# Half-block products of a SwiGLU block: token sums on VectorE, the norm hooks one step sooner, four split columns ahead of the last block product

## The chip, the cores and the metric

The kernel runs on one core of a Trainium2 chip. TensorE (PE) does the matrix products, VectorE (DVE), ScalarE (ACT) and GpSimd (POOL) the elementwise work, SyncE (SP) and GpSimd issue transfers. The metric is device microseconds of one execution; three runs of the kernel before were timed.

## The reference, cut to what matters

Two layers work on 512 tokens of width 1024 in float32. Layer 0 mixes tokens with a convolution module, layer 1 with native sparse attention; each mixer is followed by a SwiGLU feed-forward block, and the change lies in that block alone:

```python
h = rmsnorm(x, norm_ffn[i])                      # x: 512 tokens x 1024
gate, up = jnp.split(h @ w_in, 2, axis=-1)       # w_in: 1024 x 2*2816
x = x + (jax.nn.silu(gate) * up) @ w_out         # w_out: 2816 x 1024
```

## The kernel before, in words

Activations lie transposed: eight tiles `x[0..7]` of 128 channels x 512 tokens. Every float32 product is made of three rounded ones: each operand is split into a high part and a remainder, and PE computes high x high, low x high and high x low (L255, L256, L257 for whole tiles, L773 for half blocks). Weights come as 160 units of at most 128x1024 (`wr`, three buffers). ScalarE rounds a unit into `wh` (L195), VectorE takes the remainder into `wl` (L204); both have two buffers, so unit i+2 is rounded only when PE has used unit i for the last time.

The block (`ffn`, once a layer) has these stages.

- **Start.** Four units (27 to 30 in layer 0) make four projection tiles. The sum of squares over channels was gathered in `acc`; `norm_1` puts it on PE (`ssq`, L315) and takes a reciprocal root on VectorE, `norm_2` spreads it over the partitions (`rbc`, L324) and copies it to `R` (L327). The pair of numbers `FFN_H` says behind which of the eight half-unit steps each hook is written.
- **Whole tiles.** Units 31 to 38 make gate and up of four more tiles of hidden channels; `act` evacuates them (L688 to L692), and `divide` splits the result into `ah` (L673) and `al` (L674). Meanwhile `operand(c)`, c = 0 to 3, prepares the half-block products: the normed tokens of channel tiles c and c+4 go to `z` (L703), four halves of 256 tokens called b11, b12, b21, b22, and from them come four sums t1 to t4 in `zt` (L708 to L711, on GpSimd). All seven blocks are split into `bh` and `bl` (L714 to L718).
- **Pairs.** The other 16 hidden tiles take seven products of half blocks each, instead of eight (`pair`, L773); GpSimd adds the weight sums (L747, L748) and issues their transfers (L736, L740).
- **Output.** `out_mm(m, fs)` multiplies split columns fs of the hidden tiles by the output weights of channel tile m. The units stand in the order (0,0), (1,0), (0,1), (1,1), (0,2), (1,2), (2,0) and so on, tile m and block b of at most eight columns; (0,2) and (1,2) have six columns, so 18 matmuls each. In layer 0 they are units 54 to 59, and (2,0) is unit 60. Behind block 2 of a tile comes its residual add (L920; L925 in layer 1), and in layer 0 its split for the next layer, `hh` on ScalarE (L289) and `hl` on VectorE (L290). The last product of the last pair (`tail(q)`, half block 6) stands among the first `out_mm` calls. It writes over a PSUM half that VectorE reads first (L798, in `finish`).

A scheduler sets the order of each engine's queue from the written order and its own estimate of readiness; queues then run strictly in order. Operations passed to `pe(...)` keep their written order, and so does what goes through `held(...)` while `hold[0]` is true (`w_hi`, `w_lo`, `mm3`, `divide`). `hold` is set before the output stage and, before the change, cleared behind the last product of tile 1.

Of the kernel before, what the change touches and what calls it, by code (L numbers as in the profile page):

```python
# [15 lines left out]
ALU = mybir.AluOpType  # L16
# [4 lines left out]
T = 512  # L21
# [61 lines left out]
Q2B = 3  # L83


FFN_H = (1, 3)
NREG = 6
NST = NF - NREG
NB = 7
# [19 lines left out]
def trunk(ctx: ExitStack, tc: tile.TileContext, A, out):  # L109
    nc = tc.nc  # L110
# [64 lines left out]
    hold = [False]  # L175
# [464 lines left out]
    def ffn(acc, gnext, layer, between=None):  # L640
# [9 lines left out]
        with ExitStack() as cx:  # L650
# [49 lines left out]
            def operand(c):  # L700
                z, zt = (sw.tile([P, 2 * T], F32, tag="gagb"[c % 2 * 2:][:2] + e, name=nm("z")) for e in "hl")
                for i in range(2):
                    nc.vector.scalar_tensor_tensor(z[:, i * T:(i + 1) * T], x[c + 4 * i], v(gcol + c + 4 * i), R,  # L703
                                                   ALU.mult, ALU.mult)
                b11, b12, b21, b22 = (z[:, i * H:(i + 1) * H] for i in range(4))
                t1, t2, t3, t4 = (zt[:, i * H:(i + 1) * H] for i in range(4))
                gp = nc.gpsimd
                gp.tensor_tensor(t1, b11, b12, ALU.subtract)  # L708
                gp.tensor_tensor(t2, t1, b22, ALU.add)
                gp.tensor_tensor(t4, b21, t2, ALU.subtract)  # L710
                gp.tensor_tensor(t3, b12, b22, ALU.subtract)  # L711
                h_ = sb.tile([P, NB * H], F32R, tag=f"bh{c}", name=nm("bh"))
                l_ = sb.tile([P, NB * H], F32R, tag=f"bl{c}", name=nm("bl"))
                nc.scalar.activation(h_[:, :H], b11, AF.Copy, scale=-1.0)  # L714
                nc.vector.scalar_tensor_tensor(l_[:, :H], b11, -1.0, h_[:, :H], ALU.mult, ALU.subtract)
                for d, e in ((slice(H, 3 * H), z[:, T:]), (slice(3 * H, NB * H), zt)):
                    nc.scalar.activation(h_[:, d], e, AF.Copy)
                    nc.vector.tensor_tensor(l_[:, d], e, h_[:, d], ALU.subtract)  # L718
                bh.append(h_)
                bl.append(l_)  # L720
# [46 lines left out]
            def product(ps, w, i, b, first, last):  # L767
                wh, wl = w
                for c in range(4):
                    k = slice(i * T + c * P, i * T + (c + 1) * P)  # L770
                    t = slice(b * H, (b + 1) * H)
                    for q, (p_, m_) in enumerate(((wh, bh), (wh, bl), (wl, bh))):
                        pe(nc.tensor.matmul(ps[:, :H], p_[:, k], m_[c][:, t], start=first and c == 0 and q == 0,  # L773
                                            stop=last and c == 3 and q == 2, skip_group_check=True))
# [25 lines left out]
            def pair(n, prev):  # L800
                q = dict(n=n, a=bank())
                last = n == NST - 1
                w1 = next_w(False)
                product(q["a"], w1, 0, 0, True, True)
                if prev:
                    finish(prev)
                s_g2(n)
                s_acc(n + 2)
                s_add(n + 1)
                s_load(n + 2)  # L810
                s_pre(n + 3)
                q["d"] = bank()
                product(q["d"], part[n, "ga"], 0, 3, True, True)
                c1 = copied(q["a"], "c1")
                post = tail(prev) if prev else None
                q["c5"] = copied(q["d"], "c5")
                if post:
                    post()
                w_hi(state["next"])
                w_lo()  # L820
                product(q["a"], part[n, "ga"], 1, 4, False, True)
                s_part(n, "gc", raw[n])
                b = bank()
                product(b, w1, 1, 1, True, True)
                c2 = copied(q["a"], "c2")
                s_g1(n + 1)
                if last:
                    product(q["a"], part[n, "gb"], 0, 5, False, True)
                product(q["d"], part[n, "gb"], 1, 2, False, True)
                g = q["g"] = ft.tile([P, T], F32, tag="g", name=nm("g"))  # L830
                pe(nc.vector.tensor_tensor(g[:, :H], b[:, :H], c1, ALU.subtract))
                if not last:
                    product(q["a"], part[n, "gb"], 0, 5, False, True)
                pe(nc.vector.tensor_tensor(g[:, H:], q["d"][:, :H], c2, ALU.subtract))
                return q

# [38 lines left out]
                    divide(f, fo)  # L875

            hold[0] = True
            out_mm(0, (0, 1))
            w_hi(state["next"])
            w_lo()  # L880
            finish(q)
            tail(q)()
            out_mm(0, (2, 3))
            sx.close()
            fo = cx.enter_context(tc.tile_pool(name="fo", bufs=1, side="right", reuse_waits="tile"))
            parts(4, 5, 6, 7)
# [16 lines left out]
            out_mm(1, range(8, 16))  # L903
            w_lo()
            parts(19, 20, 21)
            acc = new_acc() if gnext is not None else None
            for m, b in OUT_ORDER[4:]:
                if m not in pss:
# [5 lines left out]
                out_mm(m, range(8 * b, min(8 * b + 8, NF)))  # L914
                if b < 2:
                    continue
                if m == 1:
                    hold[0] = False
                if gnext is not None:
                    nc.vector.tensor_tensor(x[m], x[m], ps, ALU.add)  # L920
                    finish_x(m, gnext, acc, fin(m))
# [847 lines left out]
```

## Time and profile before

| | |
|---|---|
| timed, median of 3 (lowest to highest) | 1284.72 us (1283.82 to 1286.34) |
| the profiled execution, its own time | 1284.19 us |
| its span, first to last instruction | 1282.4 us |
| mean granted TensorE clock | 0.995 |
| feed-forward block of layer 0, from the start | about 199 to 565 us |
| feed-forward block of layer 1 | about 915 us to the end |

All moments are microseconds from the span's start. A row of a timeline gives start, duration, engine, line, operation, output<-inputs, shapes and count; in square brackets stands the idle time of the engine just ahead of it and who ended it. Durations reach past the start of the next operation where an engine overlaps them: matmuls of 512 columns are shown at about 0.39 us and start 0.23 us apart. A row of the view of waits gives total us, times, and the longest.

### The profile page before, as it was taken

What the parts mean: (1) busy time and instruction counts of PE and PEld (TensorE: products, weight loads), DVE (VectorE), ACT (ScalarE), POOL (GpSimd) and SP (SyncE); (2) the same over time, 40 slices, a digit from 0 to 9 for tenths busy, and PEclk for the clock granted to TensorE, in tenths of its full rate; (3) what the DMA queues carried; (4) which work ended last, traced back from release to release, by engine and by line L of the source; (5) the groups of instructions that cost most, each with busy time, mean ns of one, the idle gap of its engine ahead of it and who ended that gap; (6) DMA issues with size and microseconds to landing.
All of it is one profiled execution on the core that took longest, in us unless ns stands there. A gap on an engine that the chain in (4) does not pass through costs nothing.

```text
span 1282.4 us, 20571 instructions
## 1 busy us (share of the span) xinstructions
PE 1231.7 (96%) x7943; PEld 1032.1 (80%) x7943; DVE 817.6 (64%) x1419; ACT 560.8 (44%) x1032; POOL 371.6 (29%) x419
## 2 busy tenths in 40 slices
PE   9999799899999999999998999999989999999998
PEld 6787687689999878887777776667867999997886
DVE  5996475868666544235687777663495877855321
ACT  5322353445555533233344577773344555554211
POOL 2011023425443001121332465651262444420000
PEclk9999999999999999999999899999999999999999
DMA  8758324347776132244255101002443567732331
GB/s 310 255 186 286 84 95 152 98 123 190 192 193 158 50 100 97 91 148 110 72 138 161 25 21 39 1 17 67 148 106 108 157 174 184 197 98 91 111 113 45
DMA packets 81282, 160.03 MB, mean 125 GB/s; under 512 B 36000, under 2 KB 36896, under 8 KB 79648
## 3 DMA queue, kind: packets, MB, share of 16 engines
q1 hardware_dynamic: 65808, 109.07, 27.3%
q0 software_dynamic: 15376, 49.65, 15.1%
q8 instruction: 62, 1.02, 0.3%
q14 instruction: 36, 0.29, 0.1%
HBM read 145.16 MB, written 5.28 MB: 117 GB/s over the span
## 4 chain that ended last, share of the span: by engine, by line
PE 77%; DVE 9%; DMA 3%; POOL 3%; issue 3%; ACT 2%; SPq 1%; DVEq 0%; POOLq 0%; ACTq 0%
PE st L773 25%; PE pp L257 8%; PE pp L255 8%; PE pp L256 8%; PE st L255 6%; PE st L257 6%; PE st L256 6%; PE O L1511 3%; DVE wl L204 2%; PE cpe L466 2%; PE T L1485 1%; DVE Pm L1457 1%; POOL z L708 1%; PE S L1454 1%; DVE t L1488 1%
## 5 line engine op out<-in xcount | busy, mean ns | idle before, releaser
L195 ACT ACTIVATE wh<-wr 128x1024 fp32r<-128x1024 f32 (+3 forms) x160 | 162.4, 1015 | 329.0 <-PE st L256 149.6
L204 DVE TENSOR_TENSOR wl<-wr,wh 128x1024 fp32r<-128x1024 f32 (+3 forms) x160 | 198.3, 1240 | 130.6 <-ACT wh L195 127.3
L257 PE MATMUL pp<-hh,wl 128*128 128x512 f32 x448 | 177.3, 398 | 9.8 <-DVE wl L204 9.8
L773 PE MATMUL st<-bh,sh 128*128 128x256 f32 x640 | 182.3, 285 | 1.3 <-DVE t L798 1.3
L773 PE MATMUL st<-bh,sl 128*128 128x256 f32 x640 | 181.2, 283 | 1.1 <-DVE sl L757 1.1
L255 PE MATMUL pp<-hh,wh 128*128 128x512 f32 x448 | 177.6, 399 | 3.6 <-DVE gr L413 1.9
L773 PE MATMUL st<-bl,sh 128*128 128x256 f32 x640 | 180.7, 282 | 0.0
L256 PE MATMUL pp<-hl,wh 128*128 128x512 f32 x448 | 177.4, 397 | 0.1
L255 PE MATMUL st<-ah,wh 128*128 128x512 f32 x352 | 140.3, 399 | 3.0 <-ACT wh L195 3.0
L256 PE MATMUL st<-al,wh 128*128 128x512 f32 x352 | 140.2, 398 | 0.0
L257 PE MATMUL st<-ah,wl 128*128 128x512 f32 x352 | 139.9, 398 | 0.0
L757 DVE TENSOR_TENSOR sl<-S,sh 128x512 fp32r<-128x512 f32 x128 | 103.9, 848 | 43.0 <-ACT sh L756 41.7
L773 PEld LDWEIGHTS st<-bh,sh 128*128 128x128 f32 x640 | 122.3, 191 | 2.7 <-DVE t L798 2.2
L773 PEld LDWEIGHTS st<-bh,sl 128*128 128x128 f32 x640 | 122.5, 191 | 1.5 <-DVE sl L757 1.5
L773 PEld LDWEIGHTS st<-bl,sh 128*128 128x128 f32 x640 | 122.8, 192 | 0.0
L257 PEld LDWEIGHTS pp<-hh,wl 128*128 128x128 f32 x448 | 84.2, 188 | 33.1 <-DVE wl L204 14.1
L255 PEld LDWEIGHTS pp<-hh,wh 128*128 128x128 f32 x448 | 84.3, 189 | 27.0 <-ACT wh L195 4.2
L256 PEld LDWEIGHTS pp<-hl,wh 128*128 128x128 f32 x448 | 84.4, 188 | 20.5 <-issue 1.1
L1472 POOL TENSOR_SCALAR Pm<-Pm,sm,gates 128x512 f32<-128x512 f32 (+3 forms) x128 | 80.8, 645 | 62.8 <-DVE sm L1468 49.9
L299 POOL TENSOR_TENSOR acc<-acc,sq 128x512 f32<-128x512 f32 x18 | 31.1, 1729 | 212.1 <-ACT sq L297 198.3
L1458 ACT ACTIVATE Pm<-Pm,mx 128x512 f32<-128x512 f32 (+3 forms) x128 | 71.1, 557 | 38.5 <-DVE mx L1457 33.1
L255 PEld LDWEIGHTS st<-ah,wh 128*128 128x128 f32 x352 | 66.7, 190 | 19.8 <-ACT wh L195 3.8
(281 smaller groups left out, 2514.3 us busy)
## 6 DMA issues: line engine op xcount, KB each, us to landing
S<-fw_x POOLq DMA_DIRECT2D x64, 512.0 KB, 5.8
wr<-fw_in SPq DMA_DIRECT2D x48, 512.0 KB
wr<-fw_o SPq DMA_DIRECT2D x32, 512.0 KB
bd<-bands POOLq DMA_DIRECT2D x12, 1280.0 KB, 11.4
r<-fw_x SPq DMA_DIRECT2D x32, 256.0 KB
wr<-cw_in SPq DMA_DIRECT2D x14, 512.0 KB
wr<-fw_o SPq DMA_DIRECT2D x16, 384.0 KB
wr<-fw_s SPq DMA_DIRECT2D x8, 512.0 KB
```

The source lines that it names most:

```text
L195: held(after(nc.scalar.activation(hi[:, :cols], raws[i][:, :cols], AF.Copy), pin.get(AF)))
L204: held(after(nc.vector.tensor_tensor(lo[:, :cols], raws[i][:, :cols], hi[:, :cols], ALU.subtract), pin.get(ALU)))
L255: held(nc.tensor.matmul(ps, wh, xh, start=first, stop=False))
L256: held(nc.tensor.matmul(ps, wh, xl, start=False, stop=False))
L257: held(nc.tensor.matmul(ps, wl, xh, start=False, stop=last))
L299: (eng or nc.gpsimd).tensor_tensor(acc, acc, sq, ALU.add)
L466: last["conv"] = nc.tensor.matmul(ps[e * 64:e * 64 + 16 * m, g, :], w, f[:, g0 + g, 4 - s:68 - s], start=s == 0, stop=s == 4)
L757: pe(nc.vector.tensor_tensor(l_[:, c], z, h_[:, c], ALU.subtract))
L773: pe(nc.tensor.matmul(ps[:, :H], p_[:, k], m_[c][:, t], start=first and c == 0 and q == 0, stop=last and c == 3 and q == 2, skip_group_che ...
L1458: at_[AF] = nc.scalar.activation(Pt, Pt, AF.Exp, bias=mx, scale=-1.0, accum_out=sm)
L1472: nc.gpsimd.tensor_scalar(Pt, Pt, sm[:, k:k + 1], gates[:, t + k, br * 16 + h:br * 16 + h + 1], ALU.mult, ALU.mult)
L1511: pe(nc.tensor.matmul(o[par * 64:par * 64 + 64, P * kc:], vf[br][:, kc, g], Us[par][kc], start=False, stop=last))
```

## The change

- `FFN_H` goes from (1, 3) to (0, 2): both norm hooks are written one half-unit step earlier.
- `operand` computes the sums on VectorE. One 128x512 subtraction makes t1 and t3 (the view takes b11 and b12 from one half, b12 and b22 from the other), then two of 128x256 make t2 and t4. Per block 16 GpSimd operations become 12 VectorE operations. In `zt` t3 now stands second and t2 third, so `pair` names half blocks 4 and 5 the other way round.
- Columns 0 to 3 of output tile 0 are all written ahead of `finish(q)` and the last block product; before, columns 0 and 1 stood ahead and 2 and 3 behind.
- `hold` is cleared ahead of the loop that begins with unit (0,2).

```diff
-FFN_H = (1, 3)
+FFN_H = (0, 2)
...
-                t1, t2, t3, t4 = (zt[:, i * H:(i + 1) * H] for i in range(4))
-                gp = nc.gpsimd
-                gp.tensor_tensor(t1, b11, b12, ALU.subtract)
-                gp.tensor_tensor(t2, t1, b22, ALU.add)
-                gp.tensor_tensor(t4, b21, t2, ALU.subtract)
-                gp.tensor_tensor(t3, b12, b22, ALU.subtract)
+                nc.vector.tensor_tensor(zt[:, :T].rearrange("p (a b) -> p a b", a=2),
+                                        z[:, :T].rearrange("p (a b) -> p a b", a=2),
+                                        z.rearrange("p (a b) -> p a b", a=2)[:, :, H:], ALU.subtract)
+                nc.vector.tensor_tensor(zt[:, T:T + H], zt[:, :H], b22, ALU.add)
+                nc.vector.tensor_tensor(zt[:, T + H:], b21, zt[:, T:T + H], ALU.subtract)
...
-                product(q["a"], part[n, "ga"], 1, 4, False, True)
+                product(q["a"], part[n, "ga"], 1, 5, False, True)
...
-                    product(q["a"], part[n, "gb"], 0, 5, False, True)
+                    product(q["a"], part[n, "gb"], 0, 4, False, True)
...
             hold[0] = True
-            out_mm(0, (0, 1))
+            out_mm(0, range(4))
...
             tail(q)()
-            out_mm(0, (2, 3))
...
             parts(19, 20, 21)
+            hold[0] = False
...
-                if m == 1:
-                    hold[0] = False
```

What this does to the queues is shown at two places of layer 0; layer 1 has the same moves. First VectorE, where the operands begin. `z_2162` is z of c = 0, `z_2163` its sums, `z_2252` before and `z_2251` after are z of c = 1; `wl_2072` is unit 30. Before:

```order
L715 SCALAR_TENSOR_TENSOR bl_2171<-z_2162,bh_2170 128x256
L204 TENSOR_TENSOR wl_2072<-wr_2007,wh_2071 128x1024
L718 TENSOR_TENSOR bl_2171<-z_2162,bh_2170 128x512
L715 SCALAR_TENSOR_TENSOR bl_2261<-z_2252,bh_2260 128x256
L718 TENSOR_TENSOR bl_2261<-z_2252,bh_2260 128x512
L688 TENSOR_TENSOR g_2101<-pp_1950,Rb_2039 128x512
```

Now the same stretch of VectorE's queue; lines behind L706 stand one lower in the changed file (L717 was L718, L714 was L715), and L706, L709 and L710 are the sums.

```order
L714 SCALAR_TENSOR_TENSOR bl_2170<-z_2162,bh_2169 128x256
L706 TENSOR_TENSOR z_2163<-z_2162 128x512
L204 TENSOR_TENSOR wl_2072<-wr_2007,wh_2071 128x1024
L706 TENSOR_TENSOR z_2252<-z_2251 128x512
L717 TENSOR_TENSOR bl_2170<-z_2162,bh_2169 128x512
L714 SCALAR_TENSOR_TENSOR bl_2259<-z_2251,bh_2258 128x256
L717 TENSOR_TENSOR bl_2259<-z_2251,bh_2258 128x512
L709 TENSOR_TENSOR z_2163<-z_2163,z_2162 128x256
L688 TENSOR_TENSOR g_2101<-pp_1950,Rb_2027 128x512
```

The first subtraction stands ahead of the remainder of unit 30, and one more VectorE operation ahead of the first evacuation. Twelve such rows are spread over the stretch, and the 16 rows of L708 to L711 are gone from GpSimd's queue, where the two transfers of L740 stood behind the first two of them. No matmul changes its place in this stage, and the rows of L315, L324 and the root's operations stand where they stood on PE and VectorE.

The second place is the passage from output tile 1 to output tile 2. On PE the numbered names are `wh59` and `wl59` for unit (1,2) and `wh60` for unit (2,0). Before:

```order
L255 MATMUL st_447_4621<-ah_464_4726,wh59_4781 128x512
L256 MATMUL st_447_4621<-al_465_4727,wh59_4781 128x512
L255 MATMUL st_482_4842<-ah_108_2107,wh60_4811 128x512
L256 MATMUL st_482_4842<-al_109_2108,wh60_4811 128x512
L257 MATMUL st_447_4621<-ah_464_4726,wl59_4782 128x512
```

And PE's queue after the change, from the same matmul:

```order
L255 MATMUL st_447_4617<-ah_464_4722,wh59_4777 128x512
L256 MATMUL st_447_4617<-al_465_4723,wh59_4777 128x512
L257 MATMUL st_447_4617<-ah_464_4722,wl59_4778 128x512
L255 MATMUL st_447_4617<-ah_466_4726,wh59_4777 128x512
L256 MATMUL st_447_4617<-al_467_4727,wh59_4777 128x512
```

The two matmuls of unit 60 that stood third and fourth now come behind all 18 of unit 59. ScalarE's queue at that place, before (`hh0` and `acc` read the finished x[0]):

```order
L673 ACTIVATE ah_474_4776<-y_438_4591 128x512
L195 ACTIVATE wh59_4781<-wr59_4696 128x768
L289 ACTIVATE hh0_477_4805<-x0_76,vec_74 128x512
L297 ACTIVATE acc_476_4780<-x0_76 128x512
L195 ACTIVATE wh60_4811<-wr60_4738 128x1024
```

ScalarE's queue after:

```order
L673 ACTIVATE ah_474_4772<-y_438_4593 128x512
L195 ACTIVATE wh59_4777<-wr59_4692 128x768
L195 ACTIVATE wh60_4807<-wr60_4734 128x1024
L289 ACTIVATE hh0_477_4801<-x0_76,vec_74 128x512
L297 ACTIVATE acc_476_4776<-x0_76 128x512
```

Unit 60 is rounded before ScalarE turns to x[0]. On VectorE, in the same way, the remainder of unit 59 now stands ahead of the residual add of x[0] and that of unit 60 right behind it; before, the add and `hl0` stood ahead of both. Outside the block, a few VectorE rows of the attention stage of layer 1 change places: two rows of a softmax (L1284, L1285) and a score row (L1457) of 128x512.

More of the change, by code (lines that the diff above doesn't have):

```diff
@@ L832, in pair @@
                 if not last:
-                    product(q["a"], part[n, "gb"], 0, 5, False, True)
+                    product(q["a"], part[n, "gb"], 0, 4, False, True)
                 pe(nc.vector.tensor_tensor(g[:, H:], q["d"][:, :H], c2, ALU.subtract))
```

## The prediction

> **What bounds the kernel now.** I read the page first, then PE's waits stage by stage, then the timelines of the engines named there. The page's row of busy time:
>
> ```profile
> PE 1231.7 (96%) x7943; PEld 1032.1 (80%) x7943; DVE 817.6 (64%) x1419; ACT 560.8 (44%) x1032; POOL 371.6 (29%) x419
> ```
>
> PE is the bound. The change takes no matmul away, so it can win only what PE idles, or runs slowly, in the two feed-forward blocks. PE's waits in layer 0 from 196 to 280 us, the start and whole-tile stages:
>
> ```profile
> PE pp L257 <- DVE wl L204: 4.7, 4, 1.9
> PE st L773 <- DVE sl L757: 0.5, 1, 0.5
> PE pp L255 <- ACT wh L195: 0.5, 1, 0.5
> ```
>
> Layer 1, asked from 912 to 996 us, answers with the same three rows, so what holds here holds twice. Four waits are for the remainder of a weight unit on VectorE. Why it comes late stands in VectorE's timeline:
>
> ```profile
> 215.83 3.71 DVE L703 SCALAR_TENSOR_TENSOR z<-x,vec,Rb 128x512 f32<-128x512 f32 x4 [2.69 <-ACT Rb L327]
> ...
> 220.34 5.04 DVE L204 TENSOR_TENSOR wl<-wr,wh 128x1024 fp32r<-128x1024 f32 x1
> ...
> 230.30 1.40 DVE L703 SCALAR_TENSOR_TENSOR z<-x,vec,Rb 128x512 f32<-128x512 f32 x2
> ...
> 237.56 0.41 DVE L715 SCALAR_TENSOR_TENSOR bl<-z,bh 128x256 fp32r<-128x256 f32 x1
> 237.89 0.68 DVE L718 TENSOR_TENSOR bl<-z,bh 128x512 fp32r<-128x512 f32 x1
> 238.50 0.68 DVE L692 TENSOR_TENSOR y<-y,g 128x512 f32<-128x512 f32 x1
> 239.10 1.21 DVE L204 TENSOR_TENSOR wl<-wr,wh 128x1024 fp32r<-128x1024 f32 x1
> 240.23 0.41 DVE L715 SCALAR_TENSOR_TENSOR bl<-z,bh 128x256 fp32r<-128x256 f32 x1
> ```
>
> The same remainder takes 5.04 us at 220.34 and 1.21 us at 239.10. The difference is what GpSimd did, in its own timeline:
>
> ```profile
> 221.20 1.72 POOL L708 TENSOR_TENSOR z<-z 128x256 f32<-128x256 f32 x1
> ...
> 235.98 5.87 POOL L708 TENSOR_TENSOR z<-z 128x256 f32<-128x256 f32 x1 [8.88 <-DVE bl L718]
> ```
>
> Its sums ran beside the slow remainder, and when VectorE was dense (236 to 242) the sum itself took 5.87 us. Each slows the other. The late second pair of sums then holds ScalarE, and VectorE behind it:
>
> ```profile
> 246.80 1.06 ACT L717 ACTIVATE bh<-z 128x1024 fp32r<-128x1024 f32 x1 [6.96 <-POOL z L710]
> ```
>
> So all four remainder waits lead back to the GpSimd sums: two through slow or backed-up VectorE work (1.9 and 1.62 us), one small one, and one of 0.79 us behind this hold. Two further places matter at the block's end; their rows stand with their terms.
>
> **The change part by part.** *Operand sums.* First, what the waits cost. PE's timeline, at the stage's start, at the wait that will stay, and at its end, and the groups of that stage:
>
> ```profile
> 214.91 0.48 PE L257 MATMUL pp<-hh,wl 128*128 128x512 f32 x1
> ...
> 239.25 0.50 PE L255 MATMUL pp<-hh,wh 128*128 128x512 f32 x1 [0.50 <-ACT wh L195]
> ...
> 264.38 0.39 PE L257 MATMUL pp<-hh,wl 128*128 128x512 f32 x1
> ...
> 274.14 0.39 PE L257 MATMUL pp<-hh,wl 128*128 128x512 f32 x1
> ```
>
> ```profile
> L257 PE MATMUL pp<-hh,wl 128*128 128x512 f32 x76 | 30.3, 401 | 4.7 <-DVE wl L204 4.7
> L255 PE MATMUL pp<-hh,wh 128*128 128x512 f32 x75 | 29.8, 397 | 0.5 <-ACT wh L195 0.5
> L256 PE MATMUL pp<-hl,wh 128*128 128x512 f32 x75 | 29.6, 395 | 0.0
> ```
>
> From 264.38 to 274.14 PE made 14 steps of three without a wait: 9.76 / 42 = 0.2324 us a matmul. The stage has 76 + 75 + 75 = 226 matmuls, 52.52 us at that rate; it took 274.14 + 0.23 - 214.91 = 59.46 us. So 6.94 us are lost, more than the 5.2 us of shown waits, since each wait also costs the overlap (0.16) and a slow next matmul (0.11). Of the 6.94, 0.09 belongs to the `rbc` matmuls ahead and 0.50 + 0.28 = 0.78 to the wait at 239.25. That one stays: PE's queue keeps one pair of unit 33 ahead of unit 32's third matmul, and `wh` of unit 33 waits for PE's own last use of unit 31. Removable: 6.07 us.
>
> Do the waits go? Twelve operations join VectorE: by the starts above (0.33 from one to the next for 256 columns, 0.60 for 512) four times 0.60 + 2 x 0.33, 5.1 us a block. The cover is PE's 0.23 us a matmul; I laid the new queue out row by row. VectorE starts at 215.83 and waits for nothing before unit 33, the tightest. Ahead of that remainder stand 36 operations: eight L703 (0.665 each, by the pair at 230.30), eight of 256 columns, fifteen of 512, and two splits and three remainders of 1024 (1.13 each), 5.3 + 2.7 + 9.0 + 5.65 = 22.65 us. It starts at about 238.5 and ends at 239.7. PE reaches it as its 109th matmul, 214.91 + 108 x 0.2324 + 0.78 = 240.8. That leaves about 1 us; by the same laying out units 30, 31, 32 and 34 have 2.6, 2.1, 1.7 and 3.1. ScalarE, no longer held by sums, has every other `wh` ready over 4 us ahead. If the cover went, each 0.1 us beyond the slack would cost PE 0.1 us. GpSimd keeps only transfer issues there: L740 no longer stands behind the first sums and goes out sooner; nobody needs it sooner. The 0.5 us wait for L757 stays, since its chain hangs on PE's last tile. Term: 2 x 6.07 = **12.1 us**. Bounds: 0 if the remainders stay late for another reason, 13.7 if the wait at 239.25 went too.
>
> [...]
>
> *Norm hooks.* Zero. The rows of L315 and L324 keep their places on PE, and the root's rows theirs on VectorE, so the hooks' new place in the text changes nothing that runs. Bounds: zero both ways.
>
> *Four columns ahead.* PE's timeline at the last product, and VectorE's:
>
> ```profile
> 435.10 0.40 PE L257 MATMUL st<-ah,wl 128*128 128x512 f32 x1
> 436.15 0.38 PE L773 MATMUL st<-bh,sh 128*128 128x256 f32 x1 [0.65 <-DVE t L798]
> ```
>
> ```profile
> 434.55 1.22 DVE L204 TENSOR_TENSOR wl<-wr,wh 128x1024 fp32r<-128x1024 f32 x1
> 435.68 0.42 DVE L798 TENSOR_TENSOR t<-st,c 128x256 f32<-128x256 f32 x1
> ```
>
> The product waits for L798, which ends at 436.10. Six more matmuls ahead of it last 6 x 0.23 = 1.4 us, until 436.7, so the wait is covered with 0.6 us to spare. It cost 436.15 - 435.10 - 0.23 = 0.82. What comes later: the product, by 0.6 us, and behind it on VectorE its two multiplications and the splits of columns 4 on. PE wants column 4 after the twelve matmuls of unit 55, 2.8 us behind the product's end; 0.33 + 0.33 + 0.68 = 1.3 us have it ready. Both layers: 2 x 0.82 = **1.6 us**; bounds 0 and 1.8 (with the refill).
>
> *Hold cleared sooner.* PE at the passage to tile 2, and what it waits for:
>
> ```profile
> 463.22 0.40 PE L256 MATMUL st<-al,wh 128*128 128x512 f32 x1
> 466.15 0.61 PE L255 MATMUL st<-ah,wh 128*128 128x512 f32 x1 [2.53 <-ACT wh L195]
> ...
> 469.90 0.39 PE L255 MATMUL st<-ah,wh 128*128 128x512 f32 x1
> ```
>
> ```profile
> 463.19 0.69 DVE L920 TENSOR_TENSOR x<-x,st 128x512 f32<-128x512 f32 x1 [6.43 <-PE st L257]
> ```
>
> ```profile
> 465.06 1.04 ACT L195 ACTIVATE wh<-wr 128x1024 fp32r<-128x1024 f32 x1
> ```
>
> PE's third matmul of the passage needs unit 60, which ScalarE rounded only behind the two operations on x[0]. Lost: 466.15 - 463.22 - 0.23 = 2.70. Then nine matmuls take 3.75 us instead of 2.09: 1.66 more, together 4.36. Unit 59 began one matmul before 463.22, at 462.99. After the change unit 60 is wanted behind all its 18, at 467.2; its round waits for unit 58's last use (about 463.0) and ends at about 464.0, its remainder, behind the add ending at 463.9, at 465.3. Slack 2 us, and nobody waits for the x[0] work that now stands behind. Layer 1 has no such work; its row:
>
> ```profile
> 1181.26 0.50 PE L255 MATMUL st<-ah,wh 128*128 128x512 f32 x1 [0.45 <-ACT wh L195]
> ```
>
> 0.45 + 0.28 = 0.73, removed by the same new PE order. Term: 4.36 + 0.73 = **5.1 us**; bounds 3.4 (if the slow matmuls stay) and 5.1.
>
> [...]
>
> *Elsewhere.* The attention rows that change places stand by this wait of PE:
>
> ```profile
> 720.42 0.38 PE L1454 MATMUL S<-kst,St 128*128 128x256 f32 x1 [0.47 <-DVE mx L1457]
> ```
>
> One 0.6 us row passes two others; I take 0 and keep 0.7 either way.
>
> Sum: 12.14 + 1.64 + 5.09 = 18.9 us against the profiled execution's 1284.19 us, which gives 1265.3. That execution lies 0.5 us below the median of three (1284.72), so I forecast 1265.8.
>
> **The rivals.** *VectorE runs late, a little.* If every operation held its queue for its full length, the 36 ahead of unit 33 would cost 0.08 us more each, 2.9 us; less the slack of 1.0, PE would wait 1.9 us and 0.28 for the overlap, 2.2 us a block: 1265.8 + 4.4 = 1270.2. The starts speak against it, but the slack is an estimate. 12%.
>
> *The slow matmuls stay.* Not caused by the wait: 1.66 us remain, 1267.5. For it: other waits close to 2 us did no such thing. Against: they begin exactly behind the longest wait of these blocks. 6%.
>
> *The remainders are late for another reason.* The operand term is 0, the rest stays: 1265.8 + 12.1 = 1278. Against it: each late one lies beside or behind GpSimd's sums. 4%.
>
> *Slower: VectorE becomes the bound.* Its place is the whole-tile stage. The price is bounded by the slow remainder, 5.04 / 1.21 = 4.2 times. If the twelve new operations ran at that factor, they would cost 5.1 x 3.2 = 16.3 us more a block; less the slack, 15.3 us of new PE waits, 30.6 us in both against 18.9 won: 1296.4. It decides where twice (5.1 x (f - 1) - 1.0) passes 18.9, at a factor f of 3.05. Against it: the slow rows appear only beside GpSimd's arithmetic, which is gone. 3% slower, and 3% for a factor near 3 that ends within 0.2%.
>
> **How the numbers follow.** A measurement of this kernel can tell about 0.2%, 2.6 us, from no change. My forecast has 72%, the rivals 12, 6, 4, 3 and 3. Around it, half a microsecond for the profiled run, 0.7 for the attention rows, 1.6 for the wait at 239.25 and the 1 us spread of the runs give 1262; upward the range takes in the second and third cases and some error of the first, to 1271. Outside lie the 10% of the last cases and what I mis-sized. Faster: 72 + 12 + 6 + 4 = 94%; same 3; slower 3.
>
> **What would show it.** In the changed profile the view of PE's waits from 196 to 275 us should keep one `wh` wait of 0.5 us and the 0.5 us of L757, and no `wl` wait; every 1024-wide L204 in that stage should take about 1.2 us; the new rows 0.4 and 0.7 us. No wait for L798, none of over 0.3 us in front of unit 60, no slow matmuls behind it, and PE's busy share near 97%. L315 and L324 should stand as far apart as now. Wrong would be: `wl` waits behind unit 33 (VectorE too full), a slow L204 without GpSimd, or a new wait in the pairs because their weight sums come late.

## The result and the profile after

Six runs of the changed kernel have a median of 1265.53 us (1261.84 to 1266.09), six of the kernel before 1284.49 us (1283.82 to 1286.34): ratio 0.9847, 95% interval 0.9834 to 0.986. The forecast was 1265.8 us, range 1262 to 1271. The profiled execution took 1265.84 us, its span is 1264.0 us. The page's row of busy time:

```profile
PE 1227.2 (97%) x7943; PEld 1031.7 (82%) x7943; DVE 822.5 (65%) x1443; ACT 560.5 (44%) x1032; POOL 333.1 (26%) x387
```

Twenty-four operations more on VectorE, 32 fewer on GpSimd, no matmul more or less. PE's waits in layer 0 from 196 to 275 us:

```profile
PE st L772 <- DVE sl L756: 0.5, 1, 0.5
PE pp L255 <- ACT wh L195: 0.5, 1, 0.5
```

The four waits for `wl` are gone; the two that were to stay, stayed. Layer 1 shows the same two. VectorE's timeline in that stage:

```profile
215.79 2.74 DVE L703 SCALAR_TENSOR_TENSOR z<-x,vec,Rb 128x512 f32<-128x512 f32 x4 [2.69 <-ACT Rb L327]
...
218.78 0.69 DVE L706 TENSOR_TENSOR z<-z 128x512 f32<-128x512 f32 x1
219.38 1.22 DVE L204 TENSOR_TENSOR wl<-wr,wh 128x1024 fp32r<-128x1024 f32 x1
...
222.66 0.42 DVE L709 TENSOR_TENSOR z<-z,z 128x256 f32<-128x256 f32 x1
...
238.47 1.22 DVE L204 TENSOR_TENSOR wl<-wr,wh 128x1024 fp32r<-128x1024 f32 x1
```

The remainder that took 5.04 us takes 1.22, the new rows 0.69 and 0.42. The tightest remainder, unit 33's, starts at 238.47, forecast 238.5, and ends at 239.69. PE takes it up here:

```profile
240.07 0.39 PE L255 MATMUL pp<-hh,wh 128*128 128x512 f32 x1
240.31 0.39 PE L256 MATMUL pp<-hl,wh 128*128 128x512 f32 x1
240.54 0.62 PE L257 MATMUL pp<-hh,wl 128*128 128x512 f32 x2
```

The pair of L257 is unit 32's last and unit 33's first matmul with `wl`, the latter at about 240.8: 1.1 us to spare, 1.0 forecast.

The trace lists every matmul in order, and both kernels have 7943. So a stage can be compared to a hundredth of a microsecond: take the starts of the same two numbered matmuls in both traces, at places where both do the same work. Time won by the changed kernel's profiled execution (minus: lost):

| stage | before, us | won, us | forecast |
|---|---|---|---|
| layer 0: start and whole tiles | 70.11 | 6.14 | 6.07 |
| layer 0: pairs, up to the last pair | 152.57 | -0.09 | 0 |
| layer 0: last product, passage to tile 2 | 70.09 | 5.26 | 0.82 + 4.36 |
| layer 1: start and whole tiles | 69.57 | 6.19 | 6.07 |
| layer 1: pairs, up to the last pair | 143.60 | -2.78 | 0 |
| layer 1: last product, passage to tile 2 | 81.27 | 1.92 | 0.82 + 0.73 |
| all else | 689.27 | 1.69 | 0 |
| sum | 1276.48 | 18.33 | 18.87 |

The edited stages came as forecast. A stage without an edit did not: the pairs of layer 1 lost 2.78 us, in waits for L797 (the L798 of before). The view of waits from 995 to 1155 us, PE's and GpSimd's rows:

```profile
POOL S L739 <- DMA S<-fw_x: 66.8, 12, 6.5
...
PE st L772 <- DVE t L797: 1.6, 4, 0.7
```

The four waits show 1.6 us of idle time but cost more. Behind the longest, at 1075.48 us, the next matmul starts 0.22 us on where the others of this loop start 0.12 apart, and twelve matmuls on, where PE's weight load waits for ScalarE's copy (L777), the step is 0.29; the waits at 1096.28 and 1107.17 show the same. Set beside the quickest execution of the same order (`e5_no_hooks`, below), these four places make up the 3.7 us by which the stage is longer here.

### The profile page after: what moved, and what is told of

Its sections match the earlier page's. It is cut to its first block, busy times and chain, and to the rows that moved or that the text cites. A ratio compares the mean times of both kernels' runs of the same rounds, so it can differ in the third digit from the quotient of the medians.

```text
span 1264.0 us, 20560 instructions
## 1 busy us (share of the span) xinstructions
PE 1227.2 (97%) x7943; PEld 1031.7 (82%) x7943; DVE 822.5 (65%) x1443; ACT 560.5 (44%) x1032; POOL 333.1 (26%) x387
## 4 chain that ended last, share of the span: by engine, by line
PE 71%; issue 8%; DVE 8%; POOL 6%; DMA 3%; ACT 3%; SPq 2%; DVEq 0%; POOLq 0%; ACTq 0%
PE st L772 15%; PE pp L255 9%; PE pp L257 8%; PE pp L256 8%; PE st L257 7%; PE st L255 7%; PE st L256 7%; PE O L1508 3%; PE cpe L466 2%; POOL S L747 2%; POOL S L746 1%; PE T L1482 1%; DVE Pm L1454 1%; PE S L1451 1%; POOL S L739 1%
## 5 line engine op out<-in xcount | busy, mean ns | idle before, releaser
L204 DVE TENSOR_TENSOR wl<-wr,wh 128x1024 fp32r<-128x1024 f32 (+3 forms) x160 | 190.9, 1193 | 136.2 <-ACT wh L195 132.8
L257 PE MATMUL pp<-hh,wl 128*128 128x512 f32 x448 | 176.5, 396 | 0.5 <-DVE wl L204 0.5
L257 PE MATMUL st<-ah,wl 128*128 128x512 f32 x352 | 139.6, 396 | 0.0
L756 DVE TENSOR_TENSOR sl<-S,sh 128x512 fp32r<-128x512 f32 x128 | 108.8, 887 | 42.3 <-ACT sh L755 41.0
L257 PEld LDWEIGHTS pp<-hh,wl 128*128 128x128 f32 x448 | 84.3, 188 | 20.8 <-DVE wl L204 1.5
L746 POOL TENSOR_TENSOR S<-S,wr 128x512 f32<-128x512 f32 x32 | 51.2, 1601 | 154.4 <-DMA wr<-fw_in 96.5
```

The lines of the kernel that those rows point to most:

```text
L204: held(after(nc.vector.tensor_tensor(lo[:, :cols], raws[i][:, :cols], hi[:, :cols], ALU.subtract), pin.get(ALU)))
L257: held(nc.tensor.matmul(ps, wl, xh, start=False, stop=last))
L746: pe(nc.gpsimd.tensor_tensor(t[:, :T], S[n][:, :T], w[:, :T], ALU.add))
L756: pe(nc.vector.tensor_tensor(l_[:, c], z, h_[:, c], ALU.subtract))
```

## The experiments

The first four kernels make one part of the change each on the kernel before; their chip had a median of 1283.22 us for before, over 1280.3 to 1288.76, a wider spread than the first. So each is read by its stages, compared as above.

**Sums on VectorE alone.** The edit is the diff's piece in `operand` and the two exchanged half blocks.

> The kernel before with the operand sums on VectorE (and the two product columns that swap with them) and nothing else of the change. Theory (GpSimd's sums made the remainders late, by sharing with VectorE and by holding ScalarE): the change's profile put 6.1 us into each operand stage, so 12.3 us in all, 1272.2 us; no wait for wl in either operand stage, the wait for wh of 0.5 us kept. Rival (the remainders are late for another reason, and the order of the last product or the hold did it): within 1 us of before, 1284. Rival on the second layer's pairs (the earlier end of the operand stage puts the pair loop into an unlucky phase): waits for L798 in the pairs of layer 1 of 2 us or more, 1275; theory of chance gives the 0 to 1.3 us of before.

1270.08 us, ratio 0.9893 (0.9873 to 0.9913), 13.1 us less. Won: 6.14 us in layer 0's whole-tile stage, 6.18 in layer 1's, 0.25 in layer 0's output passage, 0.00 in layer 1's. The view of PE's waits from 196 to 275 us holds the changed kernel's two rows and no third. So this part alone makes the first term. Layer 1's pairs did not lose: 0.90 us less than before, which speaks against the rival of an unlucky phase.

**Hold cleared sooner alone.**

```diff
             parts(19, 20, 21)
+            hold[0] = False
...
-                if m == 1:
-                    hold[0] = False
```

> The kernel before with the hold cleared ahead of tile 2's products and nothing else. Theory: the 2.53 us wait for unit 60 and the nine slow matmuls behind it go in layer 0 (4.36 us; the change's profile gained 4.33) and the 0.45 us wait in layer 1 (0.73), 5.1 us in all, 1279.4 us. Rival (the slow matmuls are not due to the wait): 3.4 us, 1281.1, with nine matmuls near 0.42 us still there. Rival (the x[0] work moved behind now delays the norm's sums): within 1 us of before.

1277.46 us, ratio 0.9952 (0.9933 to 0.997). Won in the output passages: 4.34 us and 0.97 us, in the whole-tile stages 0.00 and 0.07. The term was 4.36 + 0.73; layer 1's piece was under-sized by 0.24.

**Four columns ahead alone.**

```diff
-            out_mm(0, (0, 1))
+            out_mm(0, range(4))
...
-            out_mm(0, (2, 3))
```

> The kernel before with all four split columns ahead of the last block product and nothing else. Theory: the wait for L798 ahead of that product goes, 0.82 us a block by the prediction and 0.93 by the change's profile, 1.6 to 1.9 in all, 1282.7 us; the wait for unit 60 stays. Rival (the product is later, and what it releases on VectorE pushes the split of column 4 or unit 60's round by as much): 1284.5, with a new wait of 0.6 us or more behind the product.

1279.76 us, ratio 0.997 (0.9954 to 0.9985). Layer 1's passage won 0.93 us, and no new wait stands behind the product, so the rival of a pushed split is out. Layer 0's passage had won 0.93 us before the wait for unit 60, too, but 2.47 in all, which is 1.54 too many: the wait for unit 60 is still there, and the slow matmuls behind it are not. PE at that place:

```profile
463.46 0.50 PE L255 MATMUL st<-ah,wh 128*128 128x512 f32 x1 [2.54 <-ACT wh L195]
463.80 0.39 PE L256 MATMUL st<-al,wh 128*128 128x512 f32 x1
464.03 0.39 PE L257 MATMUL st<-ah,wl 128*128 128x512 f32 x1
```

The same wait, 2.54 us against 2.53, is followed by matmuls 0.23 us apart (the first after 0.34). So here a wait of that length slowed nothing behind it. The prediction had the two in one term.

The trace has the clock's changes. In before half rate stands for 3.41 us from 466.40, for 10.24 us (three times 3.41) from 701.92, and from 1282.18 past the span's end; the second and third begin 69 and 239 times 3.413 us behind the first. The changed kernel has one such stretch within its span, 10.24 us from 688.45. So the changes lie on a grid of 3.41 us. Here is busy time by the cells of that grid, in before. A row has from:to, the length, busy time and count of PE, PEld, DVE, ACT and POOL, then the granted clock, the share of DMA and GB/s:

```profile
462.99:466.40 3.41, 0.88 (x4) 0.44 (x3) 2.42 (x4) 2.19 (x3) 0.00 (x0) 1.00 0.00 0
466.40:469.81 3.41, 3.41 (x9) 2.63 (x9) 1.02 (x1) 0.00 (x0) 0.00 (x0) 0.50 0.58 171
469.81:473.23 3.42, 3.42 (x16) 2.75 (x16) 0.81 (x2) 1.22 (x2) 0.00 (x0) 1.00 0.25 98
```

And in the kernel with the four columns:

```profile
458.74:462.16 3.42, 2.18 (x10) 1.42 (x8) 0.88 (x2) 0.94 (x2) 0.00 (x0) 1.00 0.00 0
462.16:465.57 3.41, 2.11 (x9) 1.75 (x10) 2.57 (x3) 1.25 (x2) 0.00 (x0) 1.00 0.22 43
465.57:468.98 3.41, 3.41 (x17) 2.72 (x16) 0.79 (x2) 1.20 (x2) 0.00 (x0) 1.00 0.64 226
```

In before the wait fell into one cell of the grid: PE was busy for 0.88 of 3.41 us, and the next cell ran at half clock. Here the wait straddled two cells, busy for 2.18 and 2.11, and neither was followed by half clock. That made a new theory, tested below.

**Norm hooks alone.** The edit is `FFN_H = (0, 2)`.

> The kernel before with the two norm hooks two weight units sooner and nothing else. Theory: no instruction changes its place on any engine, so 1284.5 us, within 0.2%, and L315 and L324 start where they did, within 0.3 us. It also shows what one kernel's times and waits vary by from one profiled execution to the next: theory of chance has the waits for L798 in layer 1's pairs differ from the 0.7 us of before by some tenths up to 2 us; if they are the same to 0.1 us, the order and not chance sets them.

1282.79 us, ratio 0.999 (0.9974 to 1.0006), so no difference. But its profiled execution, the longest of its twelve, has a span of 1288.3 us, 5.9 more than before's, and lost 3.56 us in layer 0's pairs and 2.57 in layer 1's, with an order that is before's on every engine. PE's and GpSimd's waits from 275 to 435 us:

```profile
POOL S L740 <- DMA S<-fw_x: 73.1, 13, 6.9
...
PE st L773 <- DVE t L798: 1.1, 2, 0.8
```

So a loss in the pairs comes without any edit. The expectation's 0.7 us was misread: before's wait of 0.7 us stands ahead of the last product, behind the pairs. In the pairs of layer 1 before's execution shows no wait for L798, this one 0.6 us.

The next four start from the changed kernel; before's median there was 1284.66 us.

**The changed kernel with the hooks put back**, `FFN_H = (1, 3)`, the same order once more:

> The changed kernel with the norm hooks put back where they stood; no instruction changes its place, so it is the changed kernel once more, with a second profiled execution. 19.0 us less than before, as the changed kernel was. Theory (the 2.8 us that the changed kernel's profile lost in layer 1's pairs came by chance, as the 2.6 and 1.9 us that two of the one-part kernels lost there without any edit in that place): the loss in layer 1's pairs is another one, anywhere from 1 us of gain to 3 us of loss. Rival (the change's shorter operand stage brings the loop into an unlucky phase): again 2.5 to 3 us lost there.

1263.65 us, ratio 0.984 (0.9816 to 0.9865), 21.0 us less than before. The profiled execution lost nothing in the pairs: layer 1's took 0.95 us less than before's, 3.73 less than the changed kernel's, and the order of every engine's instructions is the same in both traces. So the loss does not belong to the order.

**GpSimd's sums beside VectorE's.**

```diff
                 nc.scalar.activation(h_[:, :H], b11, AF.Copy, scale=-1.0)
+                hf, dm = h_.bitcast(F32), ft.tile([P, H], F32, tag="c1", name=nm("dm"))
+                for _ in range(4):
+                    nc.gpsimd.tensor_tensor(dm, hf[:, :H], hf[:, :H], ALU.add)
```

> The changed kernel with four sums of 128x256 on GpSimd per operand put back beside VectorE's work, into a scratch tile that nothing reads, so that nothing waits for them but GpSimd's own next transfer issues. Theory A (GpSimd's arithmetic slows VectorE's while they run together, and that made two of the four waits): remainders L204 of 2 to 5 us again in the operand stage, and PE waits of 1.5 to 2 us for wl, 2 to 4 us lost a block, 4 to 8 in all, so 11 to 15 us less than before where the changed kernel has 19. Rival B (only the wait of ScalarE and VectorE for the sums cost time): L204 at 1.2 us, no wl waits, 19 us less than before.

1277.88 us, ratio 0.9945 (0.9925 to 0.9964), 6.8 us less than before. Sums that nobody waits for undo the first term: won against before are 0.00 us in layer 0's whole-tile stage and 0.06 in layer 1's. PE's waits from 196 to 275 us:

```profile
PE pp L257 <- DVE wl L204: 4.2, 3, 2.2
PE pp L255 <- ACT wh L195: 1.6, 1, 1.6
```

VectorE's timeline, the same operations as in the changed kernel:

```profile
217.16 3.47 DVE L703 SCALAR_TENSOR_TENSOR z<-x,vec,Rb 128x512 f32<-128x512 f32 x4 [2.69 <-ACT Rb L327]
220.55 0.84 DVE L717 SCALAR_TENSOR_TENSOR bl<-z,bh 128x256 fp32r<-128x256 f32 x1
221.31 1.10 DVE L706 TENSOR_TENSOR z<-z 128x512 f32<-128x512 f32 x1
222.33 1.63 DVE L204 TENSOR_TENSOR wl<-wr,wh 128x1024 fp32r<-128x1024 f32 x1
...
246.90 1.21 DVE L204 TENSOR_TENSOR wl<-wr,wh 128x1024 fp32r<-128x1024 f32 x1
```

While GpSimd adds, 256 columns take 0.84 us in place of 0.42, 512 take 1.10 in place of 0.69, 1024 take 1.63 in place of 1.22; the row at 246.90, with GpSimd idle, takes 1.21. So the slowing here is no factor: each operation beside the sums takes about 0.41 us more, at all three widths. Unit 33's remainder, the fourth L204 from there in both, starts 29.74 us behind the first L703 (246.90 - 217.16) in place of 22.68 (238.47 - 215.79). That is 7.06 us late, all of it in 18 rows that run beside GpSimd's 16 sums; less the 1.1 us of slack 6.0 remain, and 6.14 were lost. Theory A holds, and its price was under-sized: 12.3 us in both blocks where 4 to 8 were expected.

**Made waits of PE.** In layer 1's output stage, behind the first four columns of each unit; `tb` is a tile of zeros that VectorE writes anew two to five times while PE's second matmul waits for it:

```diff
...
+                    for i in range(2):
+                        pe(nc.tensor.matmul(ps, w[m][0][:, :P], tb, start=False, stop=False))
+                        if i == 0:
+                            for _ in range(2 + cnt_p[0] % 4):
+                                pe(nc.vector.tensor_scalar(tb, x[0], 0.0, None, ALU.mult))
+                            cnt_p[0] += 1
...
```

> The changed kernel with a made wait of PE in every one of the last 16 weight units of layer 1's output stage: PE reads a tile of zeros, VectorE writes it 2, 3, 4 or 5 times in turn (0.6 us each), and PE adds it into its sum; so the result is the same and PE waits about 1.4, 2.0, 2.6 and 3.2 us, four or more times each. Theory A (the clock is set by stretches of 3.41 us that follow one another without regard to the program, and is halved for one stretch when PE was busy in less than about half of the one before): no half clock behind the waits of 1.4 us, behind some of those of 2.0 and 2.6 and nearly all of 3.2, each time for a stretch of 3.41 us (or a multiple) that begins on the same grid, and each time after a stretch with PE under about 50% busy. Rival B (a wait of 2.5 us or longer halves it, a shorter one doesn't): all of 2.6 and 3.2, none of 2.0. Rival C (only 3.4 us without any work): none at all.

One execution, 1323.84 us; only its clock matters. Thirteen waits of 0.98 to 3.74 us came out, since part of VectorE's writes ran ahead. Two pairs of equal waits tell the theories apart:

```profile
1183.62 0.50 PE L923 MATMUL st<-tb,wh 128*128 128x512 f32 x1 [2.36 <-DVE tb L926]
...
1208.63 0.59 PE L923 MATMUL st<-tb,wh 128*128 128x512 f32 x1 [1.90 <-DVE tb L926]
...
1223.55 0.50 PE L923 MATMUL st<-tb,wh 128*128 128x512 f32 x1 [2.36 <-DVE tb L926]
...
1305.94 0.50 PE L923 MATMUL st<-tb,wh 128*128 128x512 f32 x1 [1.90 <-DVE tb L926]
```

Busy time by the grid at each of the four: the cell or the two cells that hold the wait, and the one behind:

```profile
1181.59:1185.01 3.42, 1.39 (x6) 1.17 (x7) 1.84 (x5) 0.00 (x0) 0.00 (x0) 1.00 0.12 45
1185.01:1188.42 3.41, 3.41 (x10) 2.63 (x9) 0.00 (x0) 0.41 (x1) 0.00 (x0) 0.50 0.00 0
...
1205.49:1208.90 3.41, 1.51 (x7) 0.93 (x6) 1.71 (x4) 0.00 (x0) 0.00 (x0) 1.00 0.39 115
1208.90:1212.31 3.41, 3.41 (x9) 2.67 (x9) 0.00 (x0) 0.00 (x0) 0.00 (x0) 0.50 0.00 0
...
1219.14:1222.55 3.41, 2.05 (x9) 1.32 (x7) 1.55 (x3) 1.06 (x1) 0.00 (x0) 1.00 0.00 0
1222.55:1225.97 3.42, 2.42 (x10) 1.99 (x11) 0.94 (x2) 0.00 (x0) 0.00 (x0) 1.00 0.66 230
1225.97:1229.38 3.41, 3.41 (x16) 2.76 (x15) 0.96 (x1) 0.85 (x1) 0.00 (x0) 1.00 0.02 5
...
1304.47:1307.89 3.42, 1.95 (x8) 1.62 (x9) 1.32 (x4) 0.00 (x0) 0.00 (x0) 1.00 0.00 0
1307.89:1311.30 3.41, 3.41 (x16) 2.74 (x15) 0.00 (x0) 0.00 (x0) 0.00 (x0) 1.00 0.00 0
```

Half clock came behind a wait of 1.90 us and not behind one of 2.36, so rival B is out; it came behind waits of 1.90 and 2.36 us, shorter than a cell, so rival C is out. Theory A stands in this run: cells with 1.39 and 1.51 us busy (41 and 44%) were followed by half clock, cells with 1.95 and 2.05 (57 and 60%) were not. The other nine made waits agree: behind seven cells with PE busy for 10 to 41% half clock followed, behind the two waits whose cells had 58 and 71% it did not. One such stretch lasted two cells, from 1294.23 us, though PE was busy for 80% of the first.

The grid was laid over all 14 traces and its cells counted. All 28 cells at full clock with PE busy for 44% or less were followed by half clock, among them the nine at made waits of `e7_gate` (10 to 44%), those of 18 and 26% in before and that of 38% in the changed kernel. From 45 to 55% both happened; the cells of 52 and 53% in before were followed by full clock. Above that only five cells were followed by half clock, one in each of five traces, busy for 72 or 73% by the profile: all in the same place of the attention stage, with eight matmuls of only 8 columns among the others. So the busy share as shown does not settle it alone; what else counts was not tried.

**The weight sum ahead of the transfer, in the pairs.**

```diff
-                s_acc(n + 2)
                 s_add(n + 1)
+                s_acc(n + 2)
```

> The changed kernel with GpSimd's sum of the next weight (L746, L747) put ahead of the accumulating transfer (L739) in each pair of the feed-forward blocks; no other engine's order changes. Theory (the pairs' waits for L797 come where GpSimd stands waiting for the load of S, 5.5 to 6.5 us, and its sum behind it comes late and beside VectorE's work): no waits for L797 in the pairs of either layer, and 0.5 to 3 us less than the changed kernel, 19.5 to 22 us less than before. Rival (the sum then waits for the split of the last one, and the transfer behind it comes too late for the next pair): new waits of PE for sl or t in the pairs, the time that of the changed kernel or up to 3 us more.

1289.64 us, ratio 1.005 (1.0029 to 1.007): 5.0 us more than before, 26.0 more than the changed kernel's order beside it (1263.65). The theory's forecast fell. The rival had the right mechanism, new waits of PE for `t` (L797: 6.2 us in layer 0's pairs, 5.8 in layer 1's), but allowed 3 us at most. Layer 0's pairs lost 13.03 us, layer 1's 8.94. GpSimd's timeline there:

```profile
339.78 1.29 POOL L746 TENSOR_TENSOR S<-S,wr 128x512 f32<-128x512 f32 x1 [6.46 <-issue]
341.16 1.63 POOL L747 TENSOR_TENSOR S<-S,wr 128x512 f32<-128x512 f32 x1
342.72 1.18 POOL L739 DMA_DIRECT2D S<-fw_x  x1
343.48 1.01 POOL L735 DMA_DIRECT2D S<-fw_x  x1
350.76 1.30 POOL L746 TENSOR_TENSOR S<-S,wr 128x512 f32<-128x512 f32 x1 [6.27 <-issue]
```

From one L746 to the next 10.98 us, where PE's pair lasts 10.0 (L798 comes every 10.01 us in before's layer 0). The transfer (L739) is issued behind the two sums, and the next sum reads what it brings. The profile names no releaser here; the rows give 1.38 + 1.56 us for the two sums and 8.04 from L739's start to the next sum, 10.98 together, and VectorE's L797, for which PE waits, comes every 10.98 us too (345.06, 356.04). So GpSimd's chain now sets the pace of the pairs; that the landing ends the 8.04 us is inferred from the program.

The last four share a chip with a median of 1284.3 us for before.

**The changed kernel once more.**

> The changed kernel itself on this chip, for the comparison with the three others: 19.0 us less than before; waits for L797 in layer 1's pairs of 0 to 3 us by chance.

1269.03 us, ratio 0.9868 (0.9844 to 0.9893), 15.3 us less than before; lost in the pairs are 2.22 us in layer 0 and 3.51 in layer 1 against before's profile. One of its six executions took 4184 us; the ratio leaves it out, no profile shows it, and its cause is open.

**Loads of S on SyncE's queue.**

```diff
-                    pe(nc.gpsimd.dma_start(S[n], fw_x(n)[:, :2 * T]))
+                    pe(nc.sync.dma_start(S[n], fw_x(n)[:, :2 * T]))
```

> The changed kernel with the loads of S (L735) issued by SyncE's queue in place of GpSimd's; the rows left on GpSimd and those of PE, VectorE and ScalarE keep their order. Theory (on GpSimd the chain sum, issue of the load, its landing, accumulating transfer, next sum closes on itself in 10.0 to 10.7 us beside PE's 10.0 us a pair, so the pairs wait by chance in some executions): no wait for L797 in the pairs of either layer, L739 no longer waits 5 us and more for the load, layer 1's pairs take 146.0 us or less in the profile (146.9 in before's, 149.7 in the changed kernel's), and 0.5 to 2 us less than the changed kernel in the median, 20 to 21 us less than before. Rival (the loads then stand behind weight transfers in SyncE's queue and land no sooner): as the changed kernel, or slower with waits for S.

1261.87 us, ratio 0.9832 (0.9809 to 0.9855), 7.2 us less than the changed kernel beside it where 0.5 to 2 were expected. The comparison flatters it: against the kernel before, the loads on SyncE win 22.4 us, and the changed order won 19.0, 21.0 and, here, 15.3. No wait for L797 in either layer's pairs; layer 1's took 0.95 us less than before's, 142.65 us (the expectation's 146.0 counted to a later matmul). But L739 still waits for the load, 67.3 us in layer 1, so that half of the theory fell: the loads land no sooner. What is different shows in GpSimd's timeline:

```profile
1061.20 1.20 POOL L739 DMA_DIRECT2D S<-fw_x  x1 [5.21 <-DMA S<-fw_x]
1063.32 1.29 POOL L746 TENSOR_TENSOR S<-S,wr 128x512 f32<-128x512 f32 x1 [0.92 <-DVE sl L756]
```

The sum has time left, it waits for VectorE; the load behind L739 no longer hangs on it.

**PE's order and the first splits.** The matmuls of the whole tiles go through `held` one by one with `hold` set, and `w_hi`, `w_lo` and `s_g1(0)` stand ahead of the last `act`.

> The changed kernel with PE's matmuls of the whole tiles in program order (unit 33's first pair no longer ahead of unit 32's last matmul) and the first pair's splits ahead of the last whole tile's product with the gate on VectorE and ScalarE. Theory: the 0.5 us wait for wh (0.78 us lost) and the 0.5 us wait for sl (270.53 - 269.71 - 0.12 = 0.70 us lost) go in both layers, 2 x 1.48 = 3.0 us less than the changed kernel, 22 us less than before. Rival (the wait for wh only moves, since ScalarE's round of unit 33 waits for PE's last use of unit 31 all the same): 1.4 us less, with a wait for wh at the start of unit 33.

1259.4 us, ratio 0.9807 (0.9784 to 0.9829), 24.9 us less than before, and the view of PE's waits from 196 to 435 us is empty. Won beyond the changed kernel: 1.50 us in layer 0 (7.64 - 6.14) and 1.50 in layer 1 (6.89 - 6.19, and 1.75 - 0.95 where the split's wait falls into the pairs), 3.0 as expected. Its profiled execution lost nothing in the pairs, and the changed kernel's beside it lost 5.7 us; so of its lead of 9.6 us over that kernel about 3 are its own.

**Both.**

> Both of the two: loads of S on SyncE's queue, and PE's and the splits' order. Theory: the gains add, 3.5 to 5 us less than the changed kernel. Rival (one of them failed by itself): the sum of what the two show.

1260.7 us, ratio 0.9823 (0.98 to 0.9847). The whole-tile stage's gain is there (7.65 us in layer 0), and no pair lost. It is 8.3 us below the changed kernel beside it, more than the theory's 3.5 to 5, but the two gains do not add up in the times: PE's order alone has 1259.4, and its execution had lost nothing in the pairs either.

## Why the prediction was right

**Operand sums: right in mechanism, place and size.** 12.33 us against 12.1. The unit named as tightest was the tightest, its start came within 0.03 us, and GpSimd's arithmetic was the cause: without it the waits go, and with sums beside that nobody reads the same loss comes back. The prediction gave one wait of before, 0.79 us, to the hold of ScalarE by late sums. The slower VectorE rows alone reach the whole loss in `e6_beside`; what that hold had cost in the kernel before was not separated. The rival of operations that hold their queue for their full length fell: L706 at 218.78 and L204 at 219.38 are 0.60 us apart where L706 shows 0.69. VectorE did not become the bound either: every 1024-wide remainder in the stage took 1.22 or 1.23 us, so the factor of 3.05 from which that rival decided was never near. The prediction priced it by a factor, 5.04 / 1.21; `e6_beside` shows an addition of about 0.41 us per operation, so the price would have been another.

**Norm hooks: zero**, as the same order on all engines had said; the traces of before and of the hooks alone have every instruction in the same place.

**Four columns: right, a little small.** 0.93 us in each layer by the part alone (in layer 0 up to the wait for unit 60), 1.87 in all against 1.64, at the upper bound of 1.8 that took in the refill.

**Hold: the sum right, its cause half wrong.** 5.31 us against 5.09. The wait was worth what was said, and layer 1's 0.97 in place of 0.73. The slow matmuls were put down to the wait as such, because they began behind the longest one. In the runs it went by where the wait fell on the 3.41 us grid. Of the four profiled executions that have the wait, in three it left one cell with PE busy for 26% (before), 42% (`e1_sums`) and 28% (`e4_norm`); half clock followed and cost 1.4 to 1.7 us. In the fourth, `e3_cols`, the two cells had 64 and 62%, and none followed. In `e7_gate` half clock came behind a cell with 1.90 us idle (44% busy) and not behind one with 1.47 (57%). Taking 1.7 us, between the two, as the bound, with 2.70 us lost to the wait and cells of 3.41, the wait goes without half clock when a cell's border falls into its middle 0.7 us, an estimate of 0.7 / 3.41 = 20%. So 1.66 us was a price paid in three of the four profiled executions, not in all.

**Elsewhere: the term that was mis-sized.** 0 with 0.7 either way was said, and two places left it. Attention took 1.76 us less between two of the numbered matmuls, but so it did in every other profiled execution, by 0.94 to 3.25 us, in the kernel with the order of before by 2.67: before's own execution was the slow one. And layer 1's pairs lost 2.78. The prediction had named a new wait in the pairs as a sign of being wrong; it came, not by the change. The two nearly cancel (1.69 - 2.78 - 0.09 = -1.2 with all else), so the single time hit closer than the working deserves. The same order won 21.0 and 15.3 us in its two later sets of runs, so 1265.53 against 1265.8 is in part luck; the stages bear the forecast out, the total alone would not.

**Where the pairs' loss comes from.** GpSimd's chain is closed: sum, issue of the load (L735), its landing, transfer (L739), next sum. Set the total that GpSimd waited for the load in a layer's pairs beside what the pairs lost against the quickest execution, over the 22 loops of the eleven profiles that have the chain as before. In 14 loops the wait is 44 to 54 us and the loss under 0.1 us. In eight it is 60 to 73 us, and all eight lost 0.95 to 4.5 us. In a loop without loss, here layer 1 of the changed order's second profile, the load lands sooner:

```profile
1053.64 0.61 POOL L735 DMA_DIRECT2D S<-fw_x  x1
1057.85 1.18 POOL L739 DMA_DIRECT2D S<-fw_x  x1 [3.60 <-DMA S<-fw_x]
1061.02 1.30 POOL L746 TENSOR_TENSOR S<-S,wr 128x512 f32<-128x512 f32 x1 [2.00 <-DVE sl L756]
```

In the changed kernel's first profile the same steps, and VectorE's split beside the late sum:

```profile
1061.44 0.61 POOL L735 DMA_DIRECT2D S<-fw_x  x1
1068.52 1.18 POOL L739 DMA_DIRECT2D S<-fw_x  x1 [6.47 <-DMA S<-fw_x]
1069.26 1.76 POOL L746 TENSOR_TENSOR S<-S,wr 128x512 f32<-128x512 f32 x1
```

```profile
1068.78 4.52 DVE L756 TENSOR_TENSOR sl<-S,sh 128x512 fp32r<-128x512 f32 x2 [1.08 <-ACT sh L755]
1073.55 1.21 DVE L204 TENSOR_TENSOR wl<-wr,wh 128x1024 fp32r<-128x1024 f32 x1
1075.02 0.41 DVE L797 TENSOR_TENSOR t<-st,c 128x256 f32<-128x256 f32 x1
```

With the issue taken off GpSimd the waits for the load were 67 to 74 us in all four loops and none lost anything. So in these runs the late load cost time only where the next load hung on the sum behind it. What makes a loop settle on early or late landings in one execution and not in the next stays open; in some it changes on the way (layer 1 of before: eleven waits of 4.6 to 6.0 us, then two of 3.62 and 3.67).

## What to carry to other kernels

Before a small sum goes to an idle GpSimd, look at what VectorE does at that moment. Here, beside a dense VectorE, one sum took 5.87 us where the other fifteen of the stage took 0.73 to 2.65, a remainder beside sums took 5.04 in place of 1.21, and moving twenty-four operations onto the busier engine won 12 us in two blocks. Look also at a chain of sum, transfer and next sum on one queue: here a turn of 10.98 us against PE's 10.0 cost 13 us in one layer. Where another queue can issue the transfer, let it; with the loads on SyncE none of four loops lost anything. And compare kernels by stage, from numbered matmul to numbered matmul: one execution's total here moved by 4 us and more without any edit.

## What the runs showed of the hardware

- The granted clock changed on a grid of 3.41 us that did not begin at the same place of the program: counted from the span's start, its first border lies at 2.2 us in before, 1.5 in `e1_sums`, 1.4 in `e3_cols`, 0.6 in `e7_gate` and 2.4 in the changed kernel. In the 14 traces the 28 cells at full clock with PE busy for 44% or less were followed by half clock, those of 45 to 55% by either, those above by full clock but for five cells with matmuls of 8 columns.
- VectorE beside GpSimd's 128x256 sums: 0.41 us more for each operation in `e6_beside`, whether it is 256, 512 or 1024 columns wide. In the kernel before, beside sums of two halves of `z`, 1.20 us in place of 0.68 for 512 columns, and once 5.04 in place of 1.21, while five sums began. What decides between these was not tried.
- The same 512 KB load of S ended a wait of GpSimd's that was short or long in the same program, mostly for a whole loop at a time: in layer 0 of before eleven waits of 3.56 to 3.87 us and two of 5.00 and 5.32, in layer 1 eleven of 4.59 to 5.96 and two of 3.62 and 3.67; the longest of all profiles is 7.5 (`e3_cols`).
- One order of instructions spread widely on the second chip: the kernel with the hooks alone, in before's order, took 1279.06 to 1290.12 us over twelve runs. By stages its profiled execution differed from before's ahead of layer 0's block (2.5 us more), in the pairs (6.1 more) and in attention (2.7 less).
